# Four 32-column matmuls for the later modulation sections' sums over partitions

## The chip, the cores and the metric

The kernel runs on one core of a Trainium2 chip, and nothing else runs beside it. The metric is the device time of one execution in microseconds (us); before the change the median of three runs is 2131.47 us (2123.22 to 2132.22). The engines that matter here are PE (TensorE: matmuls, with PEld for its weight loads), DVE (VectorE), ACT (ScalarE), POOL (GpSimd) and SP, whose queue issues nearly all ordinary DMAs.

## The reference, cut to what matters

One layer with two sub-layers, on 512 tokens of 1024 channels. A conditioning vector c sets six rows of 1024 numbers each (the modulation), with which the sub-layers' inputs and outputs are scaled and shifted:

```python
cond = silu(c)                                   # (1, 1024)
mod = cond @ w_ada + b_ada                       # (1, 6*1024)
sh1, sc1, g1, sh2, sc2, g2 = split(mod, 6)
h = rmsnorm(x, norm1_g) * (1 + sc1) + sh1
x = x + g1 * token_mixer(h, ...)                 # two attentions, gates, projections
h = rmsnorm(x, norm2_g) * (1 + sc2) + sh2
x = x + g2 * peer(h, ...)                        # 16 of 16384 experts for each head and token
out = rmsnorm(x, final_g)
```

The change touches `g1, sh2, sc2, g2` only, sections 2 to 5 of the modulation: four products of a vector of 1024 with a 1024 x 1024 matrix.

## The kernel before, in words

Tokens are taken in two blocks of 256 (`b` = 0 and 1). For each block there is a `mixer` (projections, two kinds of attention) and a `tail` (gates, projections, output projection, norm, query projection and top-k of the retrieval). The 256 tokens of block 0 then fetch their experts' rows one by one with indirect DMAs on POOL and multiply them on DVE (`by_rows`, L814, L842, L852), spread over what follows; the 256 tokens of block 1 go through all 16384 experts as dense matmuls (`s_part`, `v_part`, L379 and L1156), which fill the last third of the time.

Sections 0 and 1 of the modulation come first (`first_modulation`). Sections 2 to 5 are made beside the mixer of block 0, by the generator `later_modulation` (L261), which `load_unit` advances: after a set number of weight units loaded for the mixer, one step of the generator is taken. A step loads 512 KB of w_ada (`load_ada`, L200) into one of the seven buffers that the mixer's weights use as well, and DVE multiplies it with the conditioning values and adds it up, channel by channel of the partition (`mod_partial`, L208 and L210), into a tile `t` of 128 partitions x 1024 columns. There is one such tile, so the next section's first write to it waits until the section's sums are taken. After eight steps `mod_rows` (L246) sums `t` over its 128 partitions:

- it works in two halves of 512 columns; each loads 512 bias values onto one partition (L251; section 4 also 512 values of the norm's gain, L253),
- a matmul with one column of ones as its weights (L255) puts the 512 sums on partition 0 of a PSUM bank from the pool `mm` (three banks, which the mixer's projections use too),
- DVE adds the bias (L256; in section 4 it also makes (1 + sum) * gain, L258), on one partition,
- SP writes the 512 results to `mod_dr` in device memory (L259), from where the rows are read later: the tail of block 0 reads g1 (L144) and, one channel to a partition, sh2 and sc2 (L944).

The profile's name for a float32 matmul is two records, so that the eight matmuls of L255 are 16 records there, each with a weight load of its own.

The order on each engine is set by the framework, which simulates a timeline of the whole program and issues by it and by priorities; what an engine has been given it does strictly in order. SP's queue too goes in order: an issue that waits for data (as the store at L259 for DVE) holds the loads behind it. The tiles `mbr` and `mng` come from the tag `h_k`, which has two buffers.

Of the kernel before, what the change touches and what calls it, by code (L numbers as in the profile page):

```python
# [11 lines left out]
F32 = mybir.dt.float32  # L12
# [5 lines left out]
ALU = mybir.AluOpType  # L18
# [4 lines left out]
P = 128  # L23
D = 1024
# [61 lines left out]
def block(ctx, tc, x, cT, w_ada, bT, b_row, g1T, norm2_g, w_in, w_pa, w_pb, w_out, lq1, lk1, lq2, lk2,  # L86
          sublnT, rel_bias, w_q, skT, u_tab, uT, v_tab, final_g, sel, flip, out):
    nc = tc.nc
# [4 lines left out]
    fr = fr_guard.__enter__()  # L93
# [3 lines left out]
    def bank(nm, bufs):  # L97
        return lambda: pools["ps"].tile([P, 512], F32, name=nm, tag=nm, bufs=pools.get(nm, bufs))

    mm_ps, tp_ps, sc_ps, o_ps = bank("mm", 3), bank("tp", 2), bank("sc", 2), bank("ops", 1)  # L100
# [35 lines left out]
    def half(nm, tag="h_k", bufs=2):  # L136
        return fr.tile([P, T], F32, name=nm, tag=tag, bufs=bufs)
# [28 lines left out]

    ident = sb.tile([P, P], F32, name="ident")
    make_identity(nc, ident)
    ones = fr.tile([P, 1], F32, name="ones")
    nc.vector.memset(ones, 1.0)  # L170


# [71 lines left out]
    mod_dr = dr.tile([4, D], F32, name="mod_dr")  # L244

    def mod_rows(sec, t):  # L246

        for hf in range(2):
            sl = slice(512 * hf, 512 * hf + 512)
            br, ng = half("mbr")[0:1, :], half("mng")[0:1, :]  # L250
            nc.sync.dma_start(br, b_row[sec * D + 512 * hf:sec * D + 512 * hf + 512].rearrange("(a n) -> a n", a=1))  # L251
            if sec == 4:
                nc.sync.dma_start(ng, norm2_g[sl].rearrange("(a n) -> a n", a=1))  # L253
            pm = mm_ps()
            nc.tensor.matmul(pm[0:1, :], ones[:, 0:1], t[:, sl], start=True, stop=True)  # L255
            nc.vector.tensor_add(br, pm[0:1, :], br)  # L256
            if sec == 4:
                nc.vector.scalar_tensor_tensor(br, br, 1.0, ng, op0=ALU.add, op1=ALU.mult)  # L258
            nc.sync.dma_start(mod_dr[sec - 2:sec - 1, sl], br)  # L259

    def later_modulation():  # L261
        for sec in range(2, 6):
            t = fr.tile([P, 1536], F32, name="wacc", tag="tk")[:, 0:D]
            for q4 in range(4):
                for kh in range(2):
                    mod_partial(kh, t[:, 256 * q4:256 * q4 + 256], load_ada(4 * sec + q4, kh, shared("wa")))
                    yield
            mod_rows(sec, t)
# [163 lines left out]
    for i in range(5):  # L432
        t = fr.tile([P, 2, HW], F32, name=f"qz{i}", tag="qz", bufs=5)
# [805 lines left out]
```

## Time and profile before

| | |
|---|---|
| three runs, us | 2131.47, 2132.22, 2123.22 |
| the profiled execution, us | 2122.78, its span 2121.0 |
| mean granted TensorE clock | 0.955 |
| busy share of the span | PE 88%, PEld 79%, DVE 87%, ACT 45%, POOL 59% |
| chain that ended last, by engine | PE 38%, DVE 30%, DMA 11%, issue 8%, POOL 4%, ACT 2% |

The page's shares are means over stages that differ. The modulation's later sections lie between about 100 us and 302 us of the span. All starts in the rows below are us from the span's start, and durations of one instruction are ns where a row gives min/median/max and us elsewhere.

### The profile page before, as it was taken

How to read it: one execution, taken by the hardware profiler on the slowest of the kernel's cores; microseconds unless marked ns; L12 is line 12 of the kernel's file. 1: busy time of each engine (PE TensorE's matmuls, PEld its weight loads, DVE VectorE, ACT ScalarE, POOL GpSimd, SP SyncE). 2: the span in 40 equal slices, each digit the busy share in tenths (PEclk: the TensorE clock that was granted, in tenths of full speed). 3: DMA queues.
4: the chain of work that ended last, by engine and by line, in shares of the span. 5: the costliest groups of instructions: out<-in, count | busy, mean ns of one | idle time of the engine just before them, and what ended most of it. 6: DMA issues, size and time to landing. Idle time of an engine off the chain costs nothing.

```text
span 2121.0 us, 34486 instructions
## 1 busy us (share of the span) xinstructions
PE 1867.4 (88%) x12324; PEld 1665.5 (79%) x12324; DVE 1840.3 (87%) x3531; ACT 955.5 (45%) x1694; POOL 1243.6 (59%) x781
## 2 busy tenths in 40 slices
PE   6899989987788798869677888899999999999995
PEld 6899879987677687768575366788888898999985
DVE  7757766689999989999989899888899899888887
ACT  2445566443233356553332266544444454444442
POOL 2323323466667666767675757566776666665654
PEclk9999999998999999989988999999999999999998
DMA  9878765758889999989975866789898999999996
GB/s 295 269 211 249 207 191 170 212 184 263 296 273 302 312 324 319 315 292 294 324 239 179 269 190 213 258 280 322 317 330 303 331 340 335 332 337 324 336 324 227
DMA packets 369888, 587.99 MB, mean 277 GB/s; under 512 B 24962, under 2 KB 261002, under 8 KB 369716
## 3 DMA queue, kind: packets, MB, share of 16 engines
q1 hardware_dynamic: 295700, 316.79, 46.2%
q0 software_dynamic: 73728, 268.47, 36.3%
q8 instruction: 97, 1.59, 0.3%
q14 instruction: 75, 0.61, 0.1%
q10 hardware_dynamic: 288, 0.52, 0.1%
HBM read 575.13 MB, written 10.58 MB: 276 GB/s over the span
## 4 chain that ended last, share of the span: by engine, by line
PE 38%; DVE 30%; DMA 11%; issue 8%; POOL 4%; ACT 2%; POOLq 0%; DVEq 0%; SPq 0%; ACTq 0%
PE mm L379 11%; PE acc L1156 11%; PE s_ps L379 10%; DVE grow L842 9%; DMA grow<-in_v_tab_dram,ids 5%; DVE one L1173 3%; PE ga L871 2%; DMA grow<-in_u_tab_dram,ids 2%; POOL grow L814 2%; POOL elo L291 1%; DMA wa<-in_w_ada_dram 1%; DVE wl_k L291 1%; PE ops L533 1%; DVE wacc L210 1%; DVE one L1167 1%
## 5 line engine op out<-in xcount | busy, mean ns | idle before, releaser
L814 POOL DMA_INDIRECT grow<-in_v_tab_dram,ids x256 | 331.3, 1294 | 291.0 <-DVE elo L291 56.3
L814 POOL DMA_INDIRECT grow<-in_u_tab_dram,ids x256 | 328.7, 1284 | 209.9 <-DVE grow L842 63.0
L842 DVE SCALAR_TENSOR_TENSOR grow<-grow,h 128x1024 f32<-128x1024 f32 x256 | 359.0, 1411 | 12.8 <-DMA grow<-in_u_tab_dram,ids 9.5
L290 ACT CAST ehi<-eraw 128x1024 fp32r<-128x1024 f32 x145 | 152.6, 1052 | 214.8 <-PE s_ps L379 68.2
L852 DVE SCALAR_TENSOR_TENSOR ga<-grow,act,ga 128x1024 f32<-128x1024 f32 x127 | 162.7, 1281 | 45.1 <-DMA grow<-in_v_tab_dram,ids 44.7
L290 ACT CAST more<-eraw 128x1024 fp32r<-128x1024 f32 x111 | 116.6, 1051 | 145.4 <-PE acc L1156 52.3
L379 PEld LDWEIGHTS s_ps<-h2T,more 128*128 128x128 f32 x1320 | 166.4, 191 | 5.0 <-POOL more L291 0.2
L1156 PE MATMUL acc<-more,w 128*128 128x512 f32 x672 | 164.4, 394 | 6.5 <-DVE w L291 5.8
L379 PE MATMUL s_ps<-h2T,more 128*128 128x256 f32 x1320 | 168.1, 283 | 0.0
L1156 PE MATMUL acc<-ehi,w 128*128 128x512 f32 x576 | 150.7, 399 | 11.9 <-DVE w L291 7.9
L1156 PEld LDWEIGHTS acc<-more,w 128*128 128x128 f32 x672 | 127.6, 190 | 34.1 <-DVE w L291 6.2
L379 PE MATMUL s_ps<-h2T,ehi 128*128 128x256 f32 x1168 | 152.3, 283 | 0.7 <-ACT G L1180 0.7
L379 PEld LDWEIGHTS s_ps<-h2T,ehi 128*128 128x128 f32 x1168 | 145.9, 192 | 1.7 <-ACT G L1180 0.9
L852 DVE SCALAR_TENSOR_TENSOR acc_rows<-grow,act,acc_rows 128x1024 f32<-128x1024 f32 x71 | 119.3, 1681 | 29.8 <-DMA grow<-in_v_tab_dram,ids 28.3
L291 DVE TENSOR_TENSOR elo<-eraw,ehi 128x1024 fp32r<-128x1024 f32 x95 | 138.1, 1454 | 7.8 <-ACT ehi L290 7.0
L1156 PEld LDWEIGHTS acc<-ehi,w 128*128 128x128 f32 x576 | 104.7, 192 | 35.3 <-DVE w L291 12.7
L291 POOL TENSOR_TENSOR elo<-eraw,ehi 128x1024 fp32r<-128x1024 f32 x50 | 127.6, 2552 | 6.8 <-ACT ehi L290 3.6
L291 DVE TENSOR_TENSOR more<-eraw,more 128x1024 fp32r<-128x1024 f32 x75 | 107.8, 1439 | 5.2 <-ACT more L290 5.1
L379 PE MATMUL mm<-wh_v,h 128*128 128x256 f32 x640 | 101.8, 311 | 9.8 <-ACT wh_v L290 8.1
L871 PE MATMUL ga<-grow,diag 128*128 128x512 f32 x224 | 102.8, 601 | 0.2 <-DMA grow<-in_v_tab_dram,ids 0.2
L379 PEld LDWEIGHTS mm<-wh_v,h 128*128 128x128 f32 x640 | 90.6, 211 | 14.7 <-ACT wh_v L290 9.7
L379 PE MATMUL mm<-h,wh_k 128*128 128x256 f32 x640 | 96.1, 302 | 6.5 <-ACT qz L454 5.4
(305 smaller groups left out, 4627.0 us busy)
## 6 DMA issues: line engine op xcount, KB each, us to landing
eraw<-in_uT_dram SPq DMA_DIRECT2D x128, 512.0 KB
eraw<-in_v_tab_dram SPq DMA_DIRECT2D x128, 512.0 KB
wa<-in_w_ada_dram SPq DMA_DIRECT2D x48, 512.0 KB
w_v<-in_w_in_dram SPq DMA_DIRECT2D x40, 512.0 KB
w_k<-in_w_in_dram SPq DMA_DIRECT2D x40, 512.0 KB
w_gl<-in_w_in_dram SPq DMA_DIRECT2D x32, 512.0 KB
w_wql<-in_w_q_dram SPq DMA_DIRECT2D x32, 512.0 KB
w_q<-in_w_in_dram SPq DMA_DIRECT2D x24, 512.0 KB
```

The costliest lines, as they stand in the source:

```text
L210: nc.vector.scalar_tensor_tensor(acc, wa[:, k, :], c, acc, op0=ALU.mult, op1=ALU.add)
L290: nc.scalar.copy(hi, src)
L291: (eng or nc.vector).tensor_sub(lo, src, hi.bitcast(F32))
L379: r = nc.tensor.matmul(out_ps, a(i, k), b(j, k), start=(n == 0), stop=(n == 3 * kt - 1))
L533: nc.tensor.matmul(po[:, n, s, :], PT[:, i * P:(i + 1) * P], vs[g][:, kb, c:c + 64], start=(b0 + i == 0), stop=(b0 + i == len(blocks) - 1) ...
L814: nc.gpsimd.indirect_dma_start(out=r, out_offset=None, in_=tab, in_offset=bass.IndirectOffsetOnAxis(ap=ids[:, s:s + 1], axis=0))
L842: nc.vector.scalar_tensor_tensor(r, r, 1.0, h2, op0=ALU.mult, op1=ALU.mult, accum_out=a)
L852: nc.vector.scalar_tensor_tensor(acc[n], r, a, acc[n], op0=ALU.mult, op1=ALU.add)
L871: nc.tensor.matmul(pe_acc[0][:, sl], dg, r[:, sl], start=(s == 0), stop=(s == NPE - 1), skip_group_check=True)
L1156: nc.tensor.matmul(acc[b][hf], w[i][:, 256 * j + P * b:256 * j + P * b + P], V[jj][:, hf, :], start=(e == 0 and i + jj == 0), stop=(e == N ...
L1167: nc.vector.tensor_tensor(o2, iota_ps[:, None, :].to_broadcast(along), key2, ALU.is_equal)
L1173: nc.vector.tensor_scalar(o1[:, t, :], iota_ps, idT[:, 0, t0 + t:t0 + t + 1], idT[:, 2, t0 + t:t0 + t + 1], op0=ALU.is_equal, op1=ALU.mult)
```

## The change

`ones` becomes 32 columns wide. `mod_rows` takes the whole section at once: four matmuls, each with all 32 columns of ones as weights and 256 columns of `t`, write to partitions 0 to 31, 32 to 63, 64 to 95 and 96 to 127 of the same 256 columns of one bank, so that 32 partitions hold the same 256 sums. The bias, and the gain in section 4, are loaded in the same layout: each quarter's 256 values 32 times over, a tile of 128 x 256. One addition (and one more operation in section 4) of 128 x 256 follows, and one store takes partitions 0, 32, 64 and 96.

```diff
-    ones = fr.tile([P, 1], F32, name="ones")
+    ones = fr.tile([P, 32], F32, name="ones")
...
     def mod_rows(sec, t):
-        for hf in range(2):
-            sl = slice(512 * hf, 512 * hf + 512)
-            br, ng = half("mbr")[0:1, :], half("mng")[0:1, :]
-            nc.sync.dma_start(br, b_row[sec * D + 512 * hf:sec * D + 512 * hf + 512].rearrange("(a n) -> a n", a=1))
-            if sec == 4:
-                nc.sync.dma_start(ng, norm2_g[sl].rearrange("(a n) -> a n", a=1))
-            pm = mm_ps()
-            nc.tensor.matmul(pm[0:1, :], ones[:, 0:1], t[:, sl], start=True, stop=True)
-            nc.vector.tensor_add(br, pm[0:1, :], br)
-            if sec == 4:
-                nc.vector.scalar_tensor_tensor(br, br, 1.0, ng, op0=ALU.add, op1=ALU.mult)
-            nc.sync.dma_start(mod_dr[sec - 2:sec - 1, sl], br)
+        def quarters(src, off, nm):
+            r = half(nm)[:, 0:256]
+            nc.sync.dma_start(r, bass.AP(tensor=src.tensor, offset=src.offset + off, ap=[[256, 4], [0, 32], [1, 256]]))
+            return r
+        br = quarters(b_row, sec * D, "mbr")
+        ng = quarters(norm2_g, 0, "mng") if sec == 4 else None
+        pm = mm_ps()[:, 0:256]
+        for q in range(4):
+            nc.tensor.matmul(pm[32 * q:32 * q + 32, :], ones, t[:, 256 * q:256 * q + 256], start=True, stop=True,
+                             skip_group_check=True)
+        nc.vector.tensor_add(br, pm, br)
+        if sec == 4:
+            nc.vector.scalar_tensor_tensor(br, br, 1.0, ng, op0=ALU.add, op1=ALU.mult)
+        nc.sync.dma_start(mod_dr[sec - 2:sec - 1, :].rearrange("a (q n) -> (a q) n", q=4), br[0:P:32, :])
```

## Rows read from the trace of the kernel before

**Rows 1.** Busy time by stage: stretch, length, each engine's busy us (instructions), clock, DMA share, GB/s

```profile
100.00:200.00 100.00, 98.10 (x770) 92.94 (x769) 60.48 (x131) 51.17 (x95) 30.41 (x11) 0.98 0.78 234
...
600.00:800.00 200.00, 169.16 (x1150) 148.40 (x1150) 190.24 (x467) 81.05 (x139) 139.70 (x90) 0.94 0.91 311
...
1400.00:1600.00 200.00, 194.04 (x1231) 174.70 (x1230) 178.89 (x132) 92.01 (x106) 141.39 (x75) 1.00 0.89 318
```

**Rows 2.** The chain that ended last, 100 to 340 us: start, us, what

```profile
143.07 4.55 DMA wa<-in_w_ada_dram
...
190.06 1.82 PE mm L255 x4
...
201.23 0.59 DVE mbr L256
...
213.02 6.22 DMA wa<-in_w_ada_dram
...
244.54 0.68 DVE mbr L256
245.25 2.80 DVE mbr L258
...
248.75 4.15 DMA wa<-in_w_ada_dram
...
298.92 1.79 PE mm L255 x2
```

**Rows 3.** Line L255's instructions: duration ns min/median/max, first and last start, forms

```profile
L255 PEld LDWEIGHTS mm<-wacc,ones x16: 79/82/83, 139.9 to 298.8; 128*1 128x1 f32 x16
L255 PE MATMUL mm<-wacc,ones x16: 590/591/1057, 139.9 to 299.7; 128*1 128x512 f32 x16
```

**Rows 4.** Timeline around the second sum, and four 256-column records: start, us, engine, line, operation

```profile
189.99 1.88 PE L255 MATMUL mm<-wacc,ones 128*1 128x512 f32 x4
...
191.79 0.30 PEld L509 LDWEIGHTS sc<-k,qz 128*128 128x128 f32 x2 [0.86 <-issue]
...
237.97 1.03 PE L554 MATMUL sc<-kd,qz 128*128 128x256 f32 x4
```

**Rows 5.** Groups of PE by form, 100 to 340 us: count, busy us, mean ns

```profile
L554 PE MATMUL sc<-kd,qz 128*128 128x256 f32 x32 | 10.1, 414 | 1.0 <-DVE dst L555 1.0
```

**Rows 6.** DVE's lines of the change, and two nearest rows of 128x256

```profile
L256 DVE TENSOR_TENSOR mbr<-mm,mbr x8: 672/672/679, 153.3 to 300.7; 1x512 f32<-1x512 f32 x8
L258 DVE SCALAR_TENSOR_TENSOR mbr<-mbr,mng x2: 673/1735/2797, 245.2 to 254.5; 1x512 f32<-1x512 f32 x2
L539 DVE TENSOR_TENSOR oR<-ops,den x8: 407/413/426, 118.8 to 802.2; 128x256 f32<-128x256 f32 x8
L210 DVE SCALAR_TENSOR_TENSOR wacc<-wa,cs,wacc x154: 453/479/2645, 6.0 to 275.8; 128x256 f32<-128x256 f32 x154
```

**Rows 7.** Timeline: what POOL did while L258 took 2.80 us

```profile
245.12 2.38 POOL L291 TENSOR_TENSOR wl_k<-w_k,wh_k 128x1024 fp32r<-128x1024 f32 x1 [3.02 <-ACT wh_k L290]
```

**Rows 8.** SP's queue, 130 to 320 us: who waited for whom, us, times, longest

```profile
SPq L259 <- DVE mbr L256: 10.9, 4, 3.9
...
SPq L259 <- DVE wacc L208: 3.5, 1, 3.5
...
SPq L259 <- DVE dst L559: 2.6, 1, 2.6
```

**Rows 9.** SP's issues of the bias

```profile
L251 SPq DMA_DIRECT2D mbr<-in_b_row_dram x8: 245/348/388, 146.6 to 258.4; - x8
```

**Rows 10.** DMA, 130 to 320 us: packets and bytes; the queue; an issue line with its size

```profile
DMA packets 60726, 40.90 MB, mean 215 GB/s; under 512 B 3746, under 2 KB 59793, under 8 KB 60707
q1 hardware_dynamic: 60707, 40.67, 73.0%
wa<-in_w_ada_dram SPq DMA_DIRECT2D x22, 512.0 KB
```

**Rows 11.** Timeline: a bias load's issue and the addition that reads it

```profile
248.41 0.25 SPq L251 DMA_DIRECT2D mbr<-in_b_row_dram  x1
...
250.48 0.67 DVE L256 TENSOR_TENSOR mbr<-mm,mbr 1x512 f32<-1x512 f32 x1
```

**Rows 12.** Line L170, which fills the ones

```profile
L170 DVE MEMSET ones<- x1: 59/59/59, 0.8 to 0.8; 128x1 f32 x1
```

## The prediction, made before the changed kernel was run

> **What bounds the kernel now.** I read the table of busy time by stage first. The change lies between 100 and 302 us; the stage row for 100 to 200 us has PE busy 98.1 of 100 us, with DVE at 60.5 and a DMA share of 0.78 [rows 1]. Later the bound moves: DVE is busy 190.2 of 200 us between 600 and 800 us, PE 194.0 of 200 us between 1400 and 1600 us [rows 1]. A microsecond won early should therefore reach the end, because each later stage has a fixed amount of work on its busy engine and merely starts it earlier; it is lost only where the order of the work itself changes.
>
> The second view is the chain that ended last, restricted to this stage [rows 2]. It passes through the changed lines themselves: PE's L255 twice (1.82 us for the four records of one section, 1.79 us for two records of another), L256 three times (the first 0.59, the last 0.68, together 1.94 us) and L258 once (2.80 us). It also holds four waits for w_ada units (first 4.55, longest 6.22, last 4.15, together 20.3 us): PE's busy share notwithstanding, the stage runs partly at the pace of its loads. So the change has three accounts: PE, DVE and the SP queue with its loads.
>
> **PE.** Eight matmuls of 512 columns, 16 records [rows 3], become sixteen of 256 columns, 32 records. Before, one section's four records take 1.88 us in the timeline [rows 4] and 1.82 us of the chain [rows 2]; less a tail of 0.16 us that is 0.43 us for 512 columns, and 0.43 + 0.16 is the 591 ns of one alone [rows 3]. On the chain the tail counts 1.82 - 4 x 0.43 = 0.1 us. The nearest row for 256 columns is L554: four records in 1.03 us [rows 4], a pace of 0.22 us. One section after the change is eight such records.
>
> - If they run one after another, they take 8 x 0.22 + 0.1 = 1.86 us: nothing is won, since 4 x 256 columns are as many as 2 x 512.
> - If the four quarters of the array run fully beside each other, two records' time remains, 2 x 0.22 + 0.1 = 0.54 us, and each section wins 1.82 - 0.54 = 1.3 us, four sections 5.1 us.
> - At worst every record waits for its own weights and its whole latency: 0.414 us for the record alone [rows 5] and 0.08 us for a load of one column [rows 3], 8 x 0.494 = 3.95 us, a loss of 2.1 us a section, 8.5 us in all. (No row has a load of 32 columns.)
>
> No row shows two matmuls beside each other in different columns of the array. I take a value between the first two: the two records of one quarter write the same place and follow each other, and records start in order, so that only the second record of a quarter meets the first of the next. That leaves five of eight slots, 5 x 0.22 + 0.1 = 1.2 us; each section wins 0.6 us, together 2.5 us. The stage has PE at 98%, so I count all of it. The gap of 0.86 us in weight loads behind the old records [rows 4] is the last 512-column pass running out; behind a 256-column pass it should be half of it, which is already in the sum.
>
> The Trainium skill ("TensorE: Matmul & The Clock Gate", Part 3: Packing small matmuls) says that matmuls whose outputs start in different 32-partition strips run concurrently, and gives 2.38 times for three of them at 512 columns. By that page the win would be the 5.1 us of the second case; no run here shows it yet.
>
> **DVE.** L256 goes from eight operations of 0.672 us on one partition to four on 128 partitions of 256 columns; L539, of that shape and reading PSUM as well, has 0.413 us [rows 6]. That is 8 x 0.672 - 4 x 0.413 = 3.7 us less DVE work. L258 goes from two (0.673 when undisturbed) to one of 0.453 to 0.479 us, by L210's shape [rows 6]: 0.9 us less. DVE does not bound this stage, so only what lies on the chain counts: three pieces of 1.94 us, of which two would remain at 0.41 us: 1.1 us. The 2.80 us of L258 lie beside a POOL operation from 245.12 to 247.50 us [rows 7], and DVE ended right after it; the operation will meet another moment, which can be as bad or 2.3 us better. I count nothing. The wider memset of the ones was 59 ns [rows 12] and happens while the first loads are on their way: nothing.
>
> **SP and its loads.** Eight bias loads, two gain loads and eight stores become four, one and four. Each issue is about 0.35 us [rows 9], nine fewer are 3 us of SP time, hidden in a queue that mostly waits. More matters that the stores wait: SP stood at L259 for 10.9 + 3.5 + 2.6 = 17.0 us [rows 8], holding weight loads behind it. Half the stores could halve this, by 8.5 us; but most of these loads also wait for a free buffer, so that I put nothing in the sum, and keep 8.5 us as an end. Against it, each bias or gain load grows from 2 KB to 128 rows of 1 KB, 128 KB. Five of them are 0.64 MB and 640 packets, beside 40.9 MB and 60726 packets in 130 to 320 us [rows 10], 1.6%: by the 73% of 190 us that the queue was busy, 2.2 us of DMA time. Beside loads whose engines are idle a quarter of the time I count nothing; the far ends are in two of the rivals.
>
> **Sum.** 2.5 + 1.1 = 3.6 us less. The profiled execution took 2122.78 us (span 2121.0), so 2119.2 us for its like. The median of the runs is 2131.47, 0.41% above it, so the forecast is 2119.2 x 1.0041 = 2128 us.
>
> **The rivals.**
>
> - *Freed loads.* SP's waits at the stores halve and the loads behind them come that much earlier, where the chain has 20.3 us of waits for w_ada. For it: those waits [rows 2, 8]. Against: two of the waits at most can be moved by a store. Price 8.5 us more: 2122.78 - 3.6 - 8.5 = 2110.7, at the median 2119 us; with a luckier L258 2.3 us less, 2117. Faster.
> - *Serial and exposed.* The 32-column matmuls don't run beside each other and show their weight loads: 8.5 us lost on PE, 1.1 won on DVE, 2122.78 + 7.4 = 2130.2, at the median 2139 us. The change then doesn't do what its form says. Against: the old records kept a pace of 0.43 us with their loads hidden [rows 3, 4].
> - *The bias comes late.* The addition now needs 128 KB instead of 2 KB, and DVE is strictly in order: behind a waiting addition stand the w_ada products, the weight splits and the softmax operations of the mixer, and PE and SP behind those. Before, the shortest time from a bias load's issue to its addition was 2.07 us (248.41 to 250.48 [rows 11]), without a wait. A load in the full queue can take 4.15 to 6.22 us [rows 2]. If each section waits 4.15 us (6.22 - 2.07), that is 16.6 us, less the 3.6 us won: 2122.78 + 13.0 = 2135.8, at the median 2144.5 us. It decides from about 3.6 us of waiting in each section. Against: the seven other additions came later behind their loads (the first at 153.3 for a load at 146.6 [rows 6, 9]), and nearly all packets of the stage are under 2 KB as these are [rows 10].
>
> - *A narrow load.* The bias source is written as four quarters, each repeated 32 times. If such a load is dealt to four of the 16 DMA engines, each of these carries 32 KB, as for a whole 512 KB unit. At 215 GB/s with 73% of the queue's time used [rows 10], 295 GB/s, that is 1.8 us a load, 8.9 us for five, in which the weight units behind it land later: 2122.78 + 8.9 - 3.6 = 2128.1, at the median 2137 us. For it: the waits for w_ada on the chain [rows 2]. Against: a unit waits for a free buffer first, and lands in a quarter of the stage with idle DMA time.
>
> The Trainium skill ("DMA: Bandwidth & Descriptors", "Why a DMA increments its semaphore by 16 and not by 1") says that the number of engines is the largest up to 16 that divides the outermost sizes of both sides. Those are 4 and 128 here, so by that page it would be four; no row of the trace before has such a load.
>
> **How the numbers follow.** Two executions of one kernel differ here by up to 0.4%, so that 0.5% (10.7 us) is about what can be told from no change: faster means under 2120.8 us, slower above 2142.1. Forecast (2121 to 2132 us, itself within the bound): 46%. Freed loads, alone or with a luckier order: 20%, faster. The late bias: 16%, slower. The narrow load: 8%, of which 6 stay within the bound and 2 go over it. Serial and exposed: 10%, of which 6 stay within and 4 go over. So faster 0.20, same 0.58, slower 0.22. The order on all engines is made anew from a simulated timeline, which can add or take some microseconds in any case; the range therefore goes a little beyond the rivals' values, 2109 to 2150 us, and leaves out about 15%.
>
> **What would show it.** In the profile after: 32 records on the matmul's line; the eight of a section taking 1.2 us of the timeline (1.9: serial; 0.55: fully beside each other; 4: exposed). Four additions of about 0.41 us. SP's waits at the store near 8.5 us in total. An idle DVE ahead of the addition, ended by the bias load, would show the late bias. The start of the stages after 340 us should be some 4 us earlier. The prediction is wrong if the records show no overlap, if DVE waits for the bias, or if the difference arises after 340 us, in an order that the change does not touch.

## The result, and the profile after

The changed kernel takes 2138.36 us (median of 13 runs, 2131.13 to 2151.75); the kernel before took 2126.05 us beside it (13 runs, 2119.56 to 2135.64). The ratio is 1.0058, with a 95% interval of 1.0041 to 1.0075: slower by 0.58%. The forecast was 2128 us and no change that can be measured. The profiled execution took 2141.31 us (span 2139.5 us, granted clock 0.945; before 0.955). One run of all those below, of e1, took 2574.0 us at a granted clock of 0.656, where every other run has 0.939 or more; it is in no comparison.

All line numbers from the changed function on have grown by four; inside it the sum's matmul is now L258, the addition L260, the gain L262 and the store L263. The changed lines, by source line (shortest, median and longest ns, first and last start, form):

```profile
L258 PEld LDWEIGHTS mm<-wacc,ones x32: 106/108/110, 138.4 to 288.6; 128*32 128x32 f32 x32
L258 PE MATMUL mm<-wacc,ones x32: 379/391/404, 138.5 to 288.8; 128*32 128x256 f32 x32
...
L260 DVE TENSOR_TENSOR mbr<-mm,mbr x4: 418/421/424, 152.6 to 292.7; 128x256 f32<-128x256 f32 x4
...
L262 DVE SCALAR_TENSOR_TENSOR mbr<-mbr,mng x1: 413/413/413, 242.5 to 242.5; 128x256 f32<-128x256 f32 x1
...
L251 SPq DMA_DIRECT2D mbr<-in_b_row_dram x4: 538/588/678, 145.1 to 243.5; - x4
```

The first section's sum in the timeline:

```profile
138.45 0.16 PEld L258 LDWEIGHTS mm<-wacc,ones 128*32 128x32 f32 x8
138.45 0.64 PE L258 MATMUL mm<-wacc,ones 128*32 128x256 f32 x8
```

There are 32 records, as counted; but the eight of a section take 0.64 us, where four took 1.88 us [rows 4], and all eight weight loads lie within the first 0.16 us of that. The first four records start 0, 7, 14 and 20 ns from the section's first, the other four 240 to 260 ns from it, in all four sections. A record's quarter is not told in the trace; read as two passes over the four quarters, the quarters run fully beside each other. This is the case of 0.54 us with a longer tail, not the chosen one of 1.2 us.

What SP's stores waited for between 130 and 320 us (us in total, times, longest), and then, from the waits of all engines in the same stretch, PE's one new wait and DVE's for the bias:

```profile
SPq L263 <- DVE wacc L210: 5.3, 3, 3.6
...
SPq L263 <- DVE mbr L260: 3.7, 1, 3.7
```

```profile
PE mm L383 <- DVE mbr L260: 3.9, 1, 3.9
...
DVE mbr L260 <- DMA mbr<-in_b_row_dram: 0.4, 2, 0.2
```

SP waits 9.0 us at its stores, where it waited 17.0 us [rows 8] and 0.6 us more in a fourth row of that view, 17.6 us. DVE waits for the wider bias loads 0.4 us in all.

So PE gains more than was forecast, and the work behind the changed lines starts earlier. The first multiplication of a gathered row (L842 before, L846 after; a "row" here is one gather, an expert's row of 1024 for each of 128 tokens) starts at 474.7 us, before at 479.7. The 128th of the 256 comes 3.1 us early (826.5 against 829.6), and the exponentials of block 1's attention heads are some 6 us early at 800 us. Then the sign turns. The time by stage (stretch, length, busy us and instructions of PE, PEld, DVE, ACT and POOL, granted clock, DMA share, GB/s), first of after:

```profile
100.00:200.00 100.00, 99.52 (x828) 97.27 (x826) 65.15 (x134) 51.70 (x98) 29.94 (x12) 1.00 0.84 251
...
820.00:1010.00 190.00, 145.05 (x962) 131.13 (x961) 160.82 (x309) 92.15 (x204) 118.81 (x79) 0.86 0.85 276
...
960.00:980.00 20.00, 15.58 (x103) 14.71 (x103) 11.51 (x21) 6.49 (x13) 4.88 (x5) 0.72 0.63 186
```

The same view of the kernel before, for the two late stretches:

```profile
820.00:1010.00 190.00, 157.59 (x1090) 142.23 (x1088) 178.65 (x332) 97.79 (x215) 131.76 (x89) 0.91 0.92 304
...
960.00:980.00 20.00, 20.00 (x172) 20.00 (x171) 20.00 (x27) 9.06 (x14) 14.34 (x10) 1.00 0.88 279
```

From 100 to 200 us PE has 828 records in place of 770 [rows 1]; 16 of them are the sums' own, where there were 8. From 820 to 1010 us DVE, which bounds this stage, is busy 160.8 us in place of 178.7: 17.8 us less. In 960 to 980 us it is busy 11.5 of 20 us, and POOL, which fetches the rows, 4.9 in place of 14.3. No line at work there was edited.

**What happens there.** The waits of after between 935 and 990 us (who waits for whom: us in total, times, longest):

```profile
POOL grow L818 <- DVE grow L846: 18.5, 8, 5.3
ACT wh_pl L294 <- PE mm L383: 11.7, 3, 5.6
DVE grow L846 <- DMA grow<-in_u_tab_dram,ids: 9.4, 6, 3.3
...
PE tp L569 <- DVE Ld L566: 7.8, 1, 7.8
```

Before, POOL waited 10.9 us in this stretch for rows to be multiplied, and DVE not once for a row to land:

```profile
POOL grow L814 <- DVE grow L842: 10.9, 5, 3.5
```

Both waits at once mean that each waits for the other in turn. The timeline shows it (start, us, engine, line; in brackets the idle time before and what ended it):

```profile
965.73 1.15 POOL L818 DMA_INDIRECT grow<-in_u_tab_dram,ids  x1 [3.64 <-DVE grow L846]
...
970.42 1.22 DVE L846 SCALAR_TENSOR_TENSOR grow<-grow,h 128x1024 f32<-128x1024 f32 x1 [3.21 <-DMA grow<-in_u_tab_dram,ids]
...
971.92 0.94 POOL L818 DMA_INDIRECT grow<-in_u_tab_dram,ids  x1 [5.05 <-DVE grow L846]
...
976.62 1.23 DVE L846 SCALAR_TENSOR_TENSOR grow<-grow,h 128x1024 f32<-128x1024 f32 x1 [0.80 <-DMA grow<-in_u_tab_dram,ids]
...
978.12 0.94 POOL L818 DMA_INDIRECT grow<-in_u_tab_dram,ids  x1 [5.26 <-DVE grow L846]
```

A row is asked for at 965.73 us, multiplied from 970.42, and only then is the next one asked for, at 971.92: one row in 6.2 us, where DVE needs 1.2 us for it. The rows share seven buffers with the weight units, and the weights hold the others. From the issues of weight units and gathers and the ends of their last readers, the mean number of the seven between 960 and 980 us is 5.6 for weights and 1.3 for rows; before it was 3.3 and 3.3. One such weight unit in the timeline, from its load (the second of two, issued at 933.9) to its last reader:

```profile
928.39 5.88 SPq L346 DMA_DIRECT2D w_gl<-in_w_in_dram  x2
...
978.10 1.28 DVE L295 TENSOR_TENSOR wl_gl<-w_gl,wh_gl 128x1024 fp32r<-128x1024 f32 x1
```

It holds its buffer for 45 us; before, the gate units of this stretch held theirs 9 to 25 us. They stand because the products ahead of them stand: those need block 1's attention output, which comes 10.7 us later than before, though the heads were 6 us early at 800 us. First after, then before:

```profile
961.16 0.69 ACT L591 ACTIVATE obT<-tp,sg 128x512 f32<-128x512 f32 x1 [0.57 <-PE tp L589]
```

```profile
950.50 0.69 ACT L587 ACTIVATE obT<-tp,sg 128x512 f32<-128x512 f32 x1 [0.57 <-PE tp L585]
```

The heads fall behind already from 808 to 868 us, where their exponentials wait longer for DVE's small steps; first after, then before:

```profile
ACT Ld L562 <- DVE dst L560: 11.7, 6, 4.4
```

```profile
ACT Ld L558 <- DVE dst L556: 6.9, 5, 2.2
```

PE's granted clock falls too, 0.72 in place of 1.00 from 960 to 980 us. While PE stood idle for a head (the 7.8 us above, to 946.9 us), its clock fell to the lower of its two levels (1.2 GHz, not 2.4), at 943.8 us, and stayed there for 27.3 us; before, it fell at 945.7 us and stayed for 10.2. What this adds to the loss, no run tells.

In the built programs some 12,800 instructions belong to the part from block 1's mixer on. 555 of them stand in another place of their engine's queue than before, though no line there was changed. The order is written by the framework from its own simulated timeline, and other instructions in the front give another timeline. The front, up to 480 us, is ordered anew as well.

### The profile page after: what moved, and what is told of

Same layout as the page of the kernel before. It is cut to its first block, busy times and chain, and to the rows that moved or that the text cites. A ratio compares the mean times of both kernels' runs of the same rounds, so it can differ in the third digit from the quotient of the medians.

```text
span 2139.5 us, 34500 instructions
## 1 busy us (share of the span) xinstructions
PE 1872.0 (87%) x12340; PEld 1675.2 (78%) x12340; DVE 1830.8 (86%) x3526; ACT 954.7 (45%) x1694; POOL 1238.3 (58%) x781
## 5 line engine op out<-in xcount | busy, mean ns | idle before, releaser
L846 DVE SCALAR_TENSOR_TENSOR grow<-grow,h 128x1024 f32<-128x1024 f32 x256 | 368.6, 1447 | 28.8 <-DMA grow<-in_u_tab_dram,ids 21.2
L295 DVE TENSOR_TENSOR elo<-eraw,ehi 128x1024 fp32r<-128x1024 f32 x95 | 129.2, 1361 | 7.6 <-ACT ehi L294 7.6
L295 DVE TENSOR_TENSOR more<-eraw,more 128x1024 fp32r<-128x1024 f32 x75 | 116.4, 1553 | 10.6 <-ACT more L294 9.2
L383 PE MATMUL mm<-h,wh_k 128*128 128x256 f32 x640 | 101.1, 310 | 13.1 <-ACT wh_k L294 5.6
L383 PEld LDWEIGHTS mm<-h,wh_k 128*128 128x128 f32 x640 | 89.8, 209 | 18.3 <-ACT wh_k L294 6.4
```

The source lines that it names most:

```text
L295: (eng or nc.vector).tensor_sub(lo, src, hi.bitcast(F32))
L383: r = nc.tensor.matmul(out_ps, a(i, k), b(j, k), start=(n == 0), stop=(n == 3 * kt - 1))
L846: nc.vector.scalar_tensor_tensor(r, r, 1.0, h2, op0=ALU.mult, op1=ALU.mult, accum_out=a)
```

## The experiments

Two theories. Theory 1: the late order alone costs the time; the change's own work saves some. Theory 2: what the change issues costs the time. To tell them apart I needed the old late order with the change and a bad one without it. Two constants serve: MSTART (10) and MRATE (0.7) set when and how fast the later modulation is stepped; moving them also gives other late orders. Among such variants some have the late order of the kernel before but for a few instructions, with or without the change, and some share another one exactly. In this section MSTART and MRATE are all that is edited unless a diff shows more; "old" stands for the sums as before the change. Each run's first row multiplication (record 0 of 256), the time from record 127 to record 190, which spans the bad stretch, and that from record 255 to the end are taken from its one trace. What one trace is worth: after, e5 and e9 have the same order up to 480 us, and their record 0 comes at 474.7, 476.9 and 474.1 us.

| run | late order | record 0, us | 127 to 190, us | 255 to end, us | ratio to before |
|---|---|---|---|---|---|
| before | its own | 479.7 | 176.0 | 771.1 | 1 |
| after | another | 474.7 | 187.8 | 777.3 | 1.0058 |
| e1, changed | before's but for some 30 | 482.4 | 175.4 | 771.4 | 1.0028 |
| e2, old | a third | 479.8 | 187.7 | 782.0 | 1.0136 |
| e3, changed | a fourth | 479.0 | 187.9 | 769.0 | 1.0084 |
| e4, old | as e3 | 487.5 | 188.5 | 772.0 | 1.0131 |
| e5, changed, loads held | after's, moved by the hold | 476.9 | 191.7 | 773.8 | 1.0038 |
| e6, old, loads held | before's, moved by the hold | 480.3 | 179.0 | 779.2 | 1.0044 |
| e7, changed | before's but for 12 | 473.0 | 175.0 | 769.0 | 0.9970 |
| e8, old | before's but for 30 | 477.2 | 176.7 | 773.3 | 0.9976 |
| e9, changed, three ahead | after's, moved by the hold | 474.1 | 192.1 | 790.6 | 1.0115 |
| e10, changed | exactly after's | 479.0 | 188.2 | 773.8 | 1.0054 |
| e11, changed | before's but for 10 | 473.6 | 176.2 | 767.2 | 0.9959 |
| e12, old | before's but for 10 | 472.1 | 175.1 | 772.6 | 0.9970 |

**e1, the change with the old late order.**

```diff
-MSTART = 10
+MSTART = 12
```

> The changed kernel with MSTART = 12 instead of 10: the later modulation's steps start two and more weight units later, and nothing else is edited. The framework then orders the late part (block 1's mixer and all behind it, 12800 instructions) as in the kernel before, but for some 30; in the changed kernel 555 stand elsewhere. Theory 1, the late order costs the time: the change itself is worth its 5 to 8 us at 330 us, the stretch from 830 to 1150 us loses nothing against the kernel before, and the whole is 0.2 to 0.4% faster than the kernel before (2117 to 2122 where that takes 2126). Theory 2, the change's own work costs it (the wider loads, 32-column matmuls, a later consequence of their traffic): about 0.6% slower, as the changed kernel, with the same 17 us lost between 830 and 1150 us.

2131.65 us (11 runs), ratio 1.0028 [1.0013, 1.0044]. The late loss is gone, as theory 1 says: 175.4 us from record 127 to 190, and weights hold 3.7 buffers at 960 to 980 us. But the run is slower than before, not faster. In the trace its front is 2.7 us late at record 0 and 4.5 us at record 127, nearly all of the 4.7 us by which the profiled span is longer. The expectation missed that, and why this front is late is open.

**e2, a bad order without the change.**

```diff
 # in the kernel before
-MSTART = 10
+MSTART = 12
```

> The kernel before with MSTART = 12: no edit of mod_rows. Its late order differs from that of the kernel before by 776 instructions and from the changed kernel's by 257, so it is nearer to the changed kernel's. Theory 1: it shares the loss, and is 8 to 17 us slower than the kernel before (ratio 1.004 to 1.008) though its modulation is the old one, lost after 500 us. Theory 2: without the change nothing is lost, ratio 0.998 to 1.002.

2152.72 us (6 runs), ratio 1.0136 [1.0111, 1.0160], with the old sums and a front 0.1 us from that of before. Its stretch of 960 to 980 us looks like that of after: DVE at 11.7 of 20 us, POOL at 5.0.

```profile
960.00:980.00 20.00, 11.63 (x68) 10.71 (x69) 11.72 (x28) 5.33 (x11) 4.97 (x4) 0.62 0.66 215
```

Theory 2 cannot explain this loss, since nothing of the change is there. The whole loss, 28 us, is more than the 8 to 17 us expected: 11.7 us of it arise from record 127 to 190, and 10.9 us behind record 255, where the cause is open.

**e3 and e4, one late order with and without the change.** e3 is the changed kernel with MRATE = 0.75, e4 the kernel before with MRATE = 0.65.

> The changed kernel with MRATE = 0.75 instead of 0.7 (more modulation steps for each weight unit). Its late order is, instruction for instruction, that of the next kernel, which has the old mod_rows; both differ from the kernel before. Theory 1: against that kernel it is faster by the 3 to 9 us of the front, 0.15 to 0.45%, whatever both are against the kernel before. Theory 2: slower than that kernel by 0.6%.

> The kernel before with MRATE = 0.65: old mod_rows, the late order of the run above to the last instruction. Theory 1: slower than the run above by 3 to 9 us, all of it made before 400 us, and away from the kernel before by what this third order costs, either way by up to 15 us. Theory 2: within 0.2% of the kernel before.

2141.69 us, ratio 1.0084 [1.0062, 1.0106], and 2152.52 us, 1.0131 [1.0107, 1.0155]. Both lose the same in the bad stretch (187.9 and 188.5 us). e3 is 10.8 us faster than e4, a little more than expected, and 8.5 us of that are its earlier front. The two also differ in MRATE, so that this is not the change's worth alone.

**e5 and e6, the weight loads held back.** A narrower form of theory 1: SP issues five gate units ahead of the last head's bias band and values in after, three in before. The edit puts all of block 1's gate and branch loads behind these two; the half-size loads of the branches get the same line (e6: the same in the kernel before). The code is shortened here.

```diff
-        nc.sync.dma_start(raw.rearrange("p (a b) -> p a b", a=a), src)
+        with tc.issue_after(held_at[0]) if wkey[0] == "b" else ExitStack(), \
+             tc.issue_after(held_at[1]) if wkey[0] == "b" else ExitStack():
+            nc.sync.dma_start(raw.rearrange("p (a b) -> p a b", a=a), src)
...
-        nc.sync.dma_start(t[:, at:at + m * w].rearrange(
+        held_at[0] = nc.sync.dma_start(t[:, at:at + m * w].rearrange(
...
-            nc.sync.dma_start(v[:, 0:2, :], v_dr[i])
+            held_at[1] = nc.sync.dma_start(v[:, 0:2, :], v_dr[i]).ins
```

> The changed kernel; its order is the same up to about 830 us. One rule is added: on SP's queue the weight loads of block 1's gates and branches come behind the loads of the last attention head (bd<-vec_dr, v<-v_dr). In the changed kernel five w_gl loads and one w_pl load go out ahead of that head's bd (896.35 us); between 960 and 980 us weights then hold 6.4 of the seven places that they share with the gathered rows, and 1.3 are left for rows. Theory 1 (it is this queue that costs the late 17 us): the start of the stages up to 830 us stays 5 us earlier than in the kernel before, the loss from 830 to 1090 us falls from 16.8 us to between -3 and +4, weights hold under 4.5 places between 960 and 980 us, and the time is 2119 to 2129 us where the kernel before has about 2126. Theory 2 (the late order is dealt anew as a whole, and this queue is one detail of it): the loss stays at 10 us or more, 2132 us or above.

> The same rule in the kernel before, whose front is unchanged up to about 830 us. There only three w_gl loads go ahead of the last head's bd (886.78 us). Theory 1: little is to be won, -4 to +3 us, so 2122 to 2129 us. Theory 2, that the loads ahead of the head are needed to keep PE busy while it runs, so that holding them back costs: +5 us or more, 2131 us or above; e5 would then show it as well.

(The 6.4 and 3.95 buffers in these texts and in e9's were taken with some smaller loads that don't use the seven; without them they are 5.6 and 3.1.) e5: 2135.95 us, 1.0038 [1.0009, 1.0068]; e6: 2135.58 us, 1.0044 [1.0014, 1.0073]. Both miss what theory 1 expected in this form, and e6 does what theory 2 of its text expected. In e5 the crowd of weights is gone (3.1 buffers at 960 to 980 us) and the ten rows from 180 to 190 take 22.8 us again, in after 37.7. But the loss moved: nothing for the gates was loaded from 873 to 896 us, and the rows stood on POOL for 15.5 us:

```profile
888.34 1.31 POOL L818 DMA_INDIRECT grow<-in_u_tab_dram,ids  x1 [0.30 <-issue]
905.16 1.07 POOL L818 DMA_INDIRECT grow<-in_u_tab_dram,ids  x1 [15.51 <-DVE wl_gl L295]
```

So the full hold is no cure, and it costs the kernel before as well.

**e7 and e8, the old late order by another pace.** MRATE = 0.67 with the change (e7) and without it (e8).

> The change with MRATE = 0.67 in place of 0.7: its late order is that of the kernel before but for 12 instructions, its front is another one. Theory 1: the loss from 830 to 1090 us is -3 to +4 us, and the time follows the front: 2119 to 2130 us for a front 5 us early to 3 us late. The rival (what the change issues costs time in every order, as e1, which had this late order and came out 0.28% slower, might say): 2132 us or more, with the loss again after 340 us.

> The old sums with MRATE = 0.67; late order as in the kernel before but for 30 instructions. The partner of e7. Theory 1: 2123 to 2132 us, loss from 830 to 1090 us between -3 and +4, and e7 is faster than it by what e7's front is earlier at 480 us. The rival: e7 is slower than it by 0.3% or more.

e7: 2119.38 us, 0.9970 [0.9945, 0.9995]; e8: 2123.38 us, 0.9976 [0.9944, 1.0007]. e7, with the change and nearly the old late order, is a little faster than the kernel before; e1, with both as well, was not. e7's front is 4.2 us ahead of e8's and its median 4.0 us lower, though their intervals against the kernel before overlap. The stretch of e7:

```profile
820.00:1010.00 190.00, 153.25 (x1077) 138.23 (x1076) 178.51 (x330) 96.63 (x210) 132.64 (x88) 0.93 0.92 305
...
960.00:980.00 20.00, 19.95 (x167) 19.75 (x167) 19.62 (x25) 7.43 (x12) 16.07 (x11) 1.00 0.91 291
```

**e9, three units ahead.** As e5, but the first three gate units are not held (shortened).

```diff
+        held_at[2] -= wkey[0] == "b"                    # starts at 3
...
-        with tc.issue_after(held_at[0]) if wkey[0] == "b" else ExitStack(), \
+        with tc.issue_after(held_at[0]) if wkey[0] == "b" and held_at[2] < 0 else ExitStack(), \
```

> As e5, but three w_gl loads of block 1's gates may go out ahead of the last head's bd and v, as many as in the kernel before; the others come behind. e5 took the crowd of weights away between 960 and 980 us (3.95 places) and lost its time earlier instead: no weight load went out from 873 to 895 us, and the rows stood still between the 140th (869.0 us) and the 150th (912.7 us). Theory 1 (the gathered rows stop whenever the weight units crowd them out or their queue stands): with three ahead neither stall is there; weights hold under 4.5 places at 960 to 980 us, the time from the 140th to the 190th row is 135 to 143 us (before 138.4, changed 149.7, e5 152.9), and the whole is 2117 to 2129 us. Theory 2 (the late order as a whole decides and no single queue of it): 145 us or more from the 140th to the 190th row and 2131 us or above.

2153.39 us (4 runs), 1.0115 [1.0080, 1.0150]: the worst run with the change, and theory 1's narrow form fails again. The queue looks like that of before, yet the last head's band is issued at 894.45 us (before 886.78), since its heads are late, and weights again hold 5.0 buffers. 192.1 us go from record 127 to 190, and behind record 255 it takes 13.3 us more than after, which I can't explain. Theory 2 of that text, the late order as a whole, stands.

**e10, the changed late order behind another front.** MSTART = 4 with the change.

> The change with MSTART = 4: another front, but from block 1's mixer on exactly the changed kernel's order. Theory 1: the loss lies in that order, whatever the front: from the 180th to the 190th row 35 to 40 us (changed 37.7, before 22.7), 14 to 19 us lost between 830 and 1090 us, and the time 2134 to 2150 us. The rival (it was the changed front, through the times at which it hands over): 25 us or less for these ten rows and 2129 us or less.

2140.99 us (5 runs), 1.0054 [1.0035, 1.0074]. From record 180 to 190 it takes 37.9 us (after 37.7), and the same stretch starves:

```profile
820.00:1010.00 190.00, 144.72 (x958) 130.18 (x957) 161.47 (x310) 93.45 (x209) 119.40 (x79) 0.86 0.85 278
...
960.00:980.00 20.00, 11.75 (x72) 10.84 (x73) 11.55 (x26) 5.25 (x11) 4.98 (x4) 0.64 0.66 208
```

The loss goes with the order, not with the front that hands over to it.

**e11 and e12, a third front with the old late order.** MRATE = 0.90 with the change (e11) and without it (e12).

> The change with MRATE = 0.90: a third front, and the late order of the kernel before but for 10 instructions. Theory 1: 21 to 25 us from the 180th to the 190th row, -3 to +4 us lost between 830 and 1090 us, 2115 to 2132 us, by how early the front ends. The rival (e7's gain was its front's alone): a loss of 10 us or more after 830 us and 2134 us or above.

> The partner of e11: the old sums with MRATE = 0.90, late order again that of the kernel before but for 10 instructions. e11 had 2116.9 us (0.9959 of the kernel before) with its front 6.1 us early at 480 us. Theory 1 (in one and the same late order the change is worth its front, as e7 against e8: 4.2 us at 480 us and 4.0 us in the end): e12's first row multiplication comes 3 to 7 us after e11's 473.6 us, no more is lost after 830 us than -3 to +4, and e12 takes 2120 to 2126 us, 0.1 to 0.4% more than e11. The rival (the faster rate alone made e11 fast): e12 is within 2 us of e11, 2115 to 2119 us.

e11: 2116.90 us (10 runs), 0.9959 [0.9934, 0.9985], the fastest kernel of this study. e12: 2118.32 us (12 runs), 0.9970 [0.9954, 0.9987].

```profile
960.00:980.00 20.00, 19.96 (x168) 19.75 (x167) 20.00 (x23) 7.92 (x12) 16.07 (x11) 1.00 0.90 295
```

The late part of e11 goes as expected. e12 does not: it was to be 0.1 to 0.4% slower than e11 with a later front, and its front is 1.5 us earlier; the rival of that text holds, and at this pace the change is not worth anything that these runs tell. At equal constants and with nearly one late order, the change was thus followed by 4.0 us less (e7, e8) and 1.4 us less (e11, e12), both within their intervals.

**What follows.** In all six runs with nearly the late order of the kernel before (itself, e1, e7, e8, e11, e12) records 127 to 190 take 175.0 to 176.7 us. In all five with one of three other orders as the framework gave them (after, e2, e3, e4, e10) they take 187.7 to 188.5 us, with and without the change. The traces bear out the grouping: behind 520 us each engine does its instructions in e10 in after's order, and in e3 in e4's. Theory 1 is shown in this form: the late order costs some 12 us in this stretch, and the change costs nothing there. That the loss is one misplaced queue of loads is refuted twice (e5, e9).

The other half of theory 1, that the change's own work saves time in the front, is not shown. With equal constants, record 0 comes 5.0 us earlier with the change (after, before), 2.6 us later (e1, e2), 4.2 us earlier (e7, e8) and 1.5 us later (e11, e12): the front's order changes along with its work.

What stays open is which of the 555 other places starts the late loss, for no run moves one alone. Four things go with it in the traces. From 791 to 930 us the exponentials of block 1's heads lose 14 to 20 us against before in the five runs with another order, and at most 0.5 us in e1, e7, e8, e11 and e12. In DVE's queue the last head's first score operation stands behind 165 or 166 of the row multiplications in the five, and behind 160 in the six; first after, then before:

```profile
934.93 0.55 DVE L559 CUSTOM_DVE_ANT_0 Ld<-sc,bd 128x384 f32<-128x384 f32 x1
```

```profile
920.68 0.55 DVE L555 CUSTOM_DVE_ANT_0 Ld<-sc,bd 128x384 f32<-128x384 f32 x1
```

Weights hold up to 5.4 to 5.6 of the seven buffers, as a mean over 20 us, in the five, and up to 3.6 to 3.7 in the six. And PE's clock lies at its lower level for 23.9 to 27.3 us on end in the five, for 10.2 to 13.7 us in the six. So rows put ahead of the heads' steps, and a slow PE after the wait, are leads, not shown causes; in e5 the number is 158, and its rows lose the time in another way.

## Why the prediction was wrong

- **The step that failed** is the one from the front to the end, a term that the sum puts at nothing: "A microsecond won early should therefore reach the end ...; it is lost only where the order of the work itself changes". The reservation was right and was what happened; but its price was put at "some microseconds", in the range alone, and it was not made a rival. It measured 11.8 us from record 127 to 190 (187.8 against 176.0), where the whole sum was 3.6 us the other way. The whole walk of the profiled executions, after less before: -5.0 us at record 0, -3.1 at 127, +8.8 at 190, +12.4 at 255, +18.5 at the end of the span. The last step of 6 us is within what two executions of one kernel differ by: the profiled one of before lies 3.3 us under its median, that of after 3.0 us over its own; between the medians 12.3 us are lost. The last line of the prediction's tests, a difference that "arises after 340 us, in an order that the change does not touch", is the one that came true.
- **PE** was mis-sized in the other direction. The prediction took five of eight slots, 1.2 us a section and 2.5 us in all, since the two records of a quarter were to follow each other; four records start within 20 ns instead, and the other four 240 ns later. The eight took 0.64 us, 1.24 us less than before [rows 4], four times that is 5.0 us: the far bound. The Trainium skill ("TensorE: Matmul & The Clock Gate", Part 3: Packing small matmuls) says that such matmuls run concurrently, and gives 2.38 times for three; the trace agrees, with four.
- **DVE** came out as forecast: four additions of 0.421 us (forecast 0.413) and one L262 of 0.413 us (0.453 to 0.479). Its luck in L258's place was good: 0.41 us, where one had taken 2.80 us [rows 2].
- **SP** waited 9.0 us at its stores (forecast near 8.5). Whether these 8 us moved any load is not told apart from PE's share, nor from the new order of the front: together they came to 5.0 us at record 0.
- **Serial and exposed** is refuted by the 0.64 us. **The bias comes late** is refuted: 0.4 us of waiting in all. One wait of 3.9 us of PE on an addition is new. **The narrow load** is half right. In the trace's record of semaphore updates each of the five wide loads has one update about 1 us after its issue and then four; nearly all 512 KB units of w_ada have sixteen. Read as one landing for each engine, that is four engines; but the price of 8.9 us did not come, for the front was early. The wide loads landed 3.9 to 7.5 us after their issue, and DVE waited 0.4 us for them. **Freed loads**, at 2117 to 2119 us, is not shown: SP's waits halved, but no view tells what that was worth, and though e7 (2119.38) and e11 (2116.90) take that time, e12 takes 2118.32 us without the change.
- The range (2109 to 2150 us) held the time, but by luck in part: it starts from a median of three runs, 2131.47 us, where 13 runs have 2126.05. From there the sum of 3.6 us leads to 2122.4 us, and the time is 16 us above that. So too "up to 0.4%" between two executions: the 13 runs span 0.8%, and their medians tell 0.58% from nothing. The chance of slower was 0.22 and came from rivals in the front; none of them was the cause.

## What to carry to other kernels

Where a framework orders the instructions anew from a simulated timeline, a small edit early on deals a new hand to everything behind it, and its swing (here from 0.4% faster to 1.4% slower) can exceed the edit's own gain: compare the built orders first, and judge the edit among variants that share one late order. Where streams share a ring of buffers, look at who holds the buffers when an engine starves: a lockstep of "ask, wait, multiply, ask" in the timeline shows a ring with one place left. Sums over partitions are cheap as four 32-column matmuls into the four quarters of a bank: 0.64 us for 1024 columns, where two one-column matmuls took 1.88 us.

## What the runs showed of the hardware

- Four matmuls of 32 columns of weights each, into four strips of 32 partitions of one bank, have four records that start 0, 7, 14 and 20 ns from the first, and four more 240 ns later; all eight were done 0.64 us after the first start (ends are modelled). One record has 391 ns.
- Eight weight loads of 32 columns took 0.16 us of the timeline together, 108 ns each; a load of one column had 82 ns [rows 3].
- A 128 KB load that repeats four rows of 1 KB over 32 partitions each cost SP 588 ns to issue, where the 2 KB load cost 348 ns [rows 9].
- The semaphore of that 128 KB load was updated once about 1 us after the issue and then four times; nearly all 512 KB units of w_ada had sixteen updates. It landed 3.9 to 7.5 us after its issue (five loads).
